# Taking the first feature sums out of PSUM, all on VectorE, and five idle matmuls at the start of a two-branch decoder layer

## The chip, the cores and the metric

The kernel runs on one core of one Trainium2 chip. The metric is the device time of one launch in microseconds. Before the change it is 1397.15 us, the median of three runs (1396.82 to 1398.56). Durations of single instructions come from one profiled execution of the kernel before, taken by the hardware profiler.

## The reference

One decoder layer over 1040 rows of 1024 channels (16 learned tokens ahead of 1024 rows of x), in fp32:

```python
u = rmsnorm(h, mix_norm_pre[l])
proj = u @ w_in[l]
q, f_logit, i_in, g_out, v_pool, gate_a, gate_b = jnp.split(proj, cuts, axis=-1)
a = hgrn2(q, f_logit, i_in, g_out, lbs[l], hgrn_out_norm[l])
p = multiscale_pool(v_pool, pool_proj[l], pool_scale[l])
z = sigmoid(gate_a) * (a @ w_branch_hgrn[l]) + sigmoid(gate_b) * (p @ w_branch_pool[l])
h = h + rmsnorm(z @ w_out[l], mix_norm_post[l])
```

A gated MLP with a depthwise convolution follows. The change touches only the beginning: the norm of the rows, the product for `i_in` (V), the first two products for `g_out` (G), and the operands of the gates' products.

## The kernel before

**Numbers.** Every fp32 product is made of three faster ones. An operand is split into hi (a rounded copy, written by ScalarE) and lo (the rest, a subtraction on VectorE or GpSimd); TensorE adds hi·hi, hi·lo and lo·hi (L160 to L162 for V, L173, L174 and L177 for projections, L262, L263 and L265 for gates).

**Rows to features.** The rows come in nine tiles, in the order 1, 5, 2, 6, 3, 7, 0, 4, 8 of `vtiles` (tile 0 is the 16 learned rows). For each, ScalarE sums squares, VectorE multiplies by the root's reciprocal and the gain (`un`, L352), TensorE transposes 128 columns at a time into a PSUM bank (`pt`, L363), ScalarE copies it to `uhi` (L366) and VectorE subtracts to `ulo` (L368). The gain row itself is spread over the 128 partitions by two fp32 matmuls with a row of ones (`pg`, L437).

**V.** Four weight blocks `wi` are split into hi and lo (`split_wi`, L446 and L447, the lo of the second and fourth on GpSimd). Each tile then takes 24 matmuls. The first two tiles are interleaved by weight block; the later ones run one after the other, with the norm and transposes of later tiles between them.

**G.** Two projections G0 and G1 of 1026 columns in eight k steps of nine matmuls. Their weights are split on ScalarE (L136) and VectorE (L137). A sigmoid on ScalarE (L714) empties their PSUM banks.

**Gates.** The two gate matrices are computed by Strassen's scheme with seven products P1 to P7 for each unit of 256 columns. It takes four quarters of u (b11, b21, b22 and, for the sums, b12) and four sums of them, t1 to t4. With n the number of a row tile, the quarters' columns of tile n go with those of tile n + 4:

- t1 = b12 - b11, t2 = b22 - t1, t3 = t2 - b11, t4 = b21 - t2.

Each sum is made for 128 columns at a time from the hi and lo of `uhi` and `ulo` (`gate_steps`), and then spread, which is to say split again, into its hi (ScalarE, L333) and lo (VectorE, L334) in two halves. `SUMS_AT` says behind which V tile (5 to 8) or around which G projection (9 and more) the next step of which column block is put: block 0 is two columns at the front, blocks 1 to 4 are 128 columns each. A block has three steps: the sums t1 and t2; their spreads and the sums t3 and t4; their spreads.

**Order.** In this part the order on ScalarE, VectorE and TensorE is the written one (`manual_schedule`); GpSimd's is set by the scheduler. Each engine takes its queue strictly in order. The first gate products may begin when the sigmoid of G1 has emptied its banks, since PSUM is then shared out anew.

Of the kernel before, what the change touches and what calls it, by code (L numbers as in the profile page):

```python
# [12 lines left out]
ALU = mybir.AluOpType  # L13

P = 128
D = 1024
SEQ = 1024
NM = 16
# [16 lines left out]
HT = 514  # L35
EARLY = 4
EARLY_G = 2
SUMS_AT = {5: (1,), 6: (1, 2), 7: (1, 2), 8: (3, 2), 9: (3, 4, 0), 10: (3, 4, 0), 11: (4, 0)}
FM_SLOTS = 24
NRAW = 3  # L40
ZA = 4
# [15 lines left out]
def trunk_kernel(ctx: ExitStack, tc: tile.TileContext, x, meta_tokens, mix_norm_pre,  # L57
# [30 lines left out]
    def slot(n, dtype=F32, name="s"):  # L88
        return stage["fm", "p"].tile([P, n], dtype, tag="fm", name=nm(name), padded_shape=[P, L])
# [4 lines left out]
    def bank(name="ps"):  # L94
        return stage["ps", "p"].tile([P, 512], F32, tag="ps", name=nm(name))
# [14 lines left out]
    def rr(a):  # L110
        return a.bitcast(F32)
# [243 lines left out]
    def norm_rows(row, rows, gbc):  # L355
        return list(norm_steps(row, rows, gbc))[-1]

    def feature_steps(un, rows, uhi, ulo, t_at):
        for j in range(2):
            pt = bank("pt")  # L360
            for i in range(4):
                k = 4 * j + i
                pe.transpose(pt[:, i * rows : (i + 1) * rows], un[:rows, k * P : (k + 1) * P], ident[:rows, :rows])  # L363
            src = pt[:, : 4 * rows].rearrange("p (i t) -> p i t", i=4)
            h = uhi[:, 4 * j : 4 * j + 4, t_at : t_at + rows]
            act.copy(h, src)  # L366
            yield
            dve.tensor_tensor(ulo[:, 4 * j : 4 * j + 4, t_at : t_at + rows], src, rr(h), ALU.subtract)  # L368
            yield

    def to_features(*args):
        for _ in feature_steps(*args):
            pass
# [58 lines left out]
    ones1 = slot(P, name="ones1")  # L432
    dve.memset(ones1[:1], 1.0)
    g1 = slot(D, name="g1")
    gps = [bank("pg1") for _ in range(2)]
    for j in range(2):
        pe.matmul(gps[j], ones1[:1], g1row[:1, j * 512 : (j + 1) * 512], start=True, stop=True)  # L437

    wi = []

    def split_wi(raw):
        if len(wi) < 3:
            hi, lo = (wst.tile([P, 1024], F32R, tag=t, name=nm(t)) for t in ("whi", "wlo"))
        else:
            hi, lo = slot(1024, F32R, "wihi"), slot(1024, F32R, "wilo")
        act.copy(hi, raw)  # L446
        (pool_e if len(wi) % 2 else dve).tensor_tensor(lo, raw, rr(hi), ALU.subtract)  # L447
        wi.append((hi, lo))

    def v_mm(ps, t0, k):  # L450
# [12 lines left out]
    uns = {}  # L463

    def v_norm(i):
        if i < len(vtiles):
            uns[i] = norm_rows(rows_in[i], vtiles[i][1], g1)

    def v_feat(i):
        if i < len(vtiles):  # L470
            to_features(uns[i], vtiles[i][1], uhi, ulo, vtiles[i][0])

    vd = dram.tile([NCH, P, 512], F32, name="vscr")
    vmeta = const.tile([P, 512], F32, name="vmeta")
# [352 lines left out]
    def gate_steps(d):  # L827
        a, b = (slice(T0 + d.start + o, T0 + d.stop + o) for o in (0, 512))
        (b11h, b11l), (b21h, b21l), (b12h, b12l), (b22h, b22l) = (
            [rr(u[:, 4 * i : 4 * i + 4, c]) for u in (uhi, ulo)] for i, c in ((0, a), (1, a), (0, b), (1, b)))  # L830
        t1, t2 = halves_tmp(d.stop - d.start)
        pool_e.tensor_tensor(t2, b12l, b11l, ALU.subtract)
        dve.tensor_tensor(t1, b12h, b11h, ALU.subtract)
        dve.tensor_tensor(t1, t1, t2, ALU.add)
        dve.tensor_tensor(t2, b22h, t1, ALU.subtract)
        pool_e.tensor_tensor(t2, t2, b22l, ALU.add)
        yield
        put("t1", t1, d, dve, gq)
        put("t2", t2, d, dve, gq)
        dve.tensor_tensor(t1, t2, b11h, ALU.subtract)  # L840
        pool_e.tensor_tensor(t1, t1, b11l, ALU.subtract)
        dve.tensor_tensor(t2, b21h, t2, ALU.subtract)
        pool_e.tensor_tensor(t2, t2, b21l, ALU.add)
        yield
        put("t3", t1, d, dve, gq)
        put("t4", t2, d, dve, gq)
        yield
# [5 lines left out]
    vb = [bank("pv") for _ in range(2)]  # L853
    E = mybir.EngineType
    with tc.manual_schedule(engines={E.Activation, E.DVE, E.PE}):
        dve.tensor_copy(g1[:, :512], gps[0])
        n0, n1 = (norm_steps(rows_in[i], P, g1) for i in range(2))
        next(n0)
        next(n0)
        dve.tensor_copy(g1[:, 512:], gps[1])  # L860
        un0 = next(n0)
        next(n1)
        f0 = feature_steps(un0, P, uhi, ulo, vtiles[0][0])
        split_wi(raws[0])
        next(f0)
        next(f0)
        next(f0)
        next(n1)
        un1 = next(n1)
        next(f0)  # L870
        v_mm(vb[0], vtiles[0][0], 0)
        v_mm(vb[0], vtiles[0][0], 1)
        split_wi(raws[1])
        f1 = feature_steps(un1, P, uhi, ulo, vtiles[1][0])
        next(f1)
        next(f1)
        split_wi(raws[2])
        next(f1)
        next(f1)
        split_wi(raws[3])  # L880
        for i, j in ((0, 1), (1, 0), (0, 2), (1, 1), (0, 3), (1, 2), (1, 3)):
            for k in (2 * j, 2 * j + 1):
                v_mm(vb[i], vtiles[i][0], k)
        v_norm(2)
        v_norm(3)
        for i in range(2):
            v_feat(2 + i)
            v_norm(4 + i)
        for i in range(2):
            v_out(vb[i], vtiles[i][0])  # L890
        for i in range(2, len(vtiles)):
            ps = bank("pv")
            for k in range(KD):
                v_mm(ps, vtiles[i][0], k)
            if i < 5:
                v_feat(i + 2)
            if i == 5:
                v_feat(7)
                v_feat(8)
            v_norm(i + 4)  # L900
            if i == 3:
                params()
            if i == 5:
                for q in ("t2", "t1", "t3", "t4"):
                    two_halves(q)
                sums = [gate_steps(d) for d in ds]
            if i == len(vtiles) - 1:
                gl = Loader([job("G", h)[:2] + (P,) for h in range(EARLY_G)])
            for j in SUMS_AT.get(i, ()):
                next(sums[j])  # L910
            v_out(ps, vtiles[i][0])
        gates.load_first(0)
        gates.load_first(1)
        gates.ahead(2)
        for h in range(EARLY_G):
            src, n_k, xs, chunks, post = job("G", h)
            r = proj(None, 0, n_k, xs, chunks, ws=gl.next(), name="pg")
            for j in SUMS_AT.get(9 + 2 * h, ()):
                next(sums[j])
            post(r)  # L920
            if h == 0:
                gates.load_first(2)
                gates.ahead(4)
            for j in SUMS_AT.get(10 + 2 * h, ()):
                next(sums[j])

        close_pool("ps")
        open_pool("pf", 4, PSUM)
        gates.load_first(3)
        for e in range(0, EARLY, 2):  # L930
            p = gates.start_pair(e)
            for f in [f[i] for i in range(2) for f in p]:
                f()
                for j in SUMS_AT.get(13, ()) if e == 0 else ():
                    next(sums[j], None)
# [562 lines left out]
```

## Time and profile before

| | |
|---|---|
| median of three runs | 1397.15 us |
| lowest and highest | 1396.82, 1398.56 us |
| the profiled execution | 1396.61 us |
| its span, first to last instruction | 1394.9 us |
| TensorE busy | 1353.6 us, 97% |
| VectorE busy | 973.9 us, 70% |
| ScalarE busy | 565.0 us, 41% |
| GpSimd busy | 508.4 us, 36% |
| mean granted TensorE clock | 0.990 |

In the profile PE is TensorE's matmuls, PEld its weight loads, DVE VectorE, ACT ScalarE, POOL GpSimd. In a timeline a row has the start, the time from there to the end of the last of the instructions that it stands for, engine, line, operation, output and input names, shape and count; what stands in brackets is the idle time before it and the engine that ended it. Matmuls overlap, so a matmul's own time is longer than the distance to the next one. In a table of stretches each engine's busy time has its count of instructions behind it; the last three numbers are the granted clock, the share of the DMA engines' time and GB/s.

### The profile page before, as it was taken

How to read it: one execution, taken by the hardware profiler on the slowest of the kernel's cores; microseconds unless marked ns; L12 is line 12 of the kernel's file. 1: busy time of each engine (PE TensorE's matmuls, PEld its weight loads, DVE VectorE, ACT ScalarE, POOL GpSimd, SP SyncE). 2: the span in 40 equal slices, each digit the busy share in tenths (PEclk: the TensorE clock that was granted, in tenths of full speed). 3: DMA queues.
4: the chain of work that ended last, by engine and by line, in shares of the span. 5: the costliest groups of instructions: out<-in, count | busy, mean ns of one | idle time of the engine just before them, and what ended most of it. 6: DMA issues, size and time to landing. Idle time of an engine off the chain costs nothing. (4 is left out here: it accounts for less than half of the span.)

```text
span 1394.9 us, 21573 instructions
## 1 busy us (share of the span) xinstructions
PE 1353.6 (97%) x8405; PEld 1224.6 (88%) x8405; DVE 973.9 (70%) x1381; ACT 565.0 (41%) x945; POOL 508.4 (36%) x379
## 2 busy tenths in 40 slices
PE   8989999999999999999997999999999999999997
PEld 6879999999999899987777788888999988788786
DVE  6694655288975756565579888888887777654557
ACT  5443333356465463126564322222323223543343
POOL 4255331217543611051036565634567552000100
PEclk9999999999999999999998999999999999999999
DMA  6033433321111023589852577665677879966524
GB/s 245 31 100 121 138 104 108 103 73 46 33 33 33 18 76 122 182 265 316 288 172 91 148 218 214 192 173 145 161 166 188 197 194 268 365 231 201 179 71 166
DMA packets 133220, 215.21 MB, mean 154 GB/s; under 512 B 8327, under 2 KB 76523, under 8 KB 133120
## 3 DMA queue, kind: packets, MB, share of 16 engines
q1 hardware_dynamic: 121056, 189.47, 40.2%
q0 software_dynamic: 12064, 24.38, 10.3%
q8 instruction: 66, 1.08, 0.3%
q14 instruction: 34, 0.28, 0.1%
HBM read 160.84 MB, written 76.05 MB: 170 GB/s over the span
## 5 line engine op out<-in xcount | busy, mean ns | idle before, releaser
L262 PE MATMUL P<-v,whi 128*128 128x258 f32 (+2 forms) x528 | 162.6, 322 | 3.5 <-DVE g L1197 2.5
L263 PE MATMUL P<-v,whi 128*128 128x258 f32 (+2 forms) x528 | 161.6, 320 | 0.0
L265 PE MATMUL P<-v,wlo 128*128 128x258 f32 (+2 forms) x528 | 140.8, 321 | 1.1 <-DVE wlo L210 1.1
L137 POOL TENSOR_TENSOR wlo<-wraw,whi 128x1024 fp32r<-128x1024 f32 (+2 forms) x23 | 50.0, 2174 | 183.0 <-ACT whi L136 101.3
L262 PEld LDWEIGHTS P<-v,whi 128*128 128x128 f32 x528 | 100.8, 191 | 11.8 <-DVE g L1197 2.9
L263 PEld LDWEIGHTS P<-v,whi 128*128 128x128 f32 x528 | 100.7, 191 | 7.5
L161 PE MATMUL pd<-rot 128*128 128x512 f32 x272 | 106.0, 390 | 0.3 <-DVE rot L1257 0.3
L162 PE MATMUL pd<-rot 128*128 128x512 f32 x272 | 105.9, 389 | 0.0
L265 PEld LDWEIGHTS P<-v,wlo 128*128 128x128 f32 x528 | 87.9, 190 | 8.8 <-DVE wlo L210 1.3
L136 ACT CAST whi<-wraw 128x1024 fp32r<-128x1024 f32 (+2 forms) x44 | 36.2, 825 | 146.0 <-PE pba L174 31.3
L209 ACT CAST whi<-wraw 128x512 fp32r<-128x512 f32 x90 | 53.0, 617 | 101.8 <-PE P L263 83.9
L1257 DVE TENSOR_TENSOR rot<-yt,rot 128x1024 fp32r<-128x1024 f32 x33 | 41.2, 1250 | 71.0 <-ACT rot L1256 71.0
L210 DVE TENSOR_TENSOR wlo<-wraw,whi 128x512 fp32r<-128x512 f32 x82 | 75.9, 949 | 18.5 <-ACT whi L209 18.5
L1141 POOL TENSOR_TENSOR ys<-y 128x512 f32<-128x512 f32 x22 | 35.2, 1600 | 142.3 <-issue 96.8
L235 POOL TENSOR_TENSOR swa<-wraw,wraw 128x512 f32<-128x512 f32 x30 | 45.5, 1518 | 95.9 <-DMA wraw<-in_w_in_dram 62.4
L160 PE MATMUL pd<-rot 128*128 128x512 f32 x272 | 72.7, 390 | 2.0 <-ACT rot L1256 2.0
L1256 ACT CAST rot<-yt 128x1024 fp32r<-128x1024 f32 x33 | 34.6, 1053 | 90.2 <-PE pd L161 90.2
L209 ACT CAST whi<-swa 128x512 fp32r<-128x512 f32 x60 | 35.9, 619 | 86.8 <-PE P L263 71.6
L1189 DVE SCALAR_TENSOR_TENSOR y<-g,par,y 128x1024 f32<-128x1024 f32 x44 | 65.1, 1479 | 0.7
L160 PEld LDWEIGHTS pd<-rot 128*128 128x128 f32 x272 | 50.9, 188 | 13.5 <-ACT rot L1256 2.9
L210 DVE TENSOR_TENSOR wlo<-swb,whi 128x512 fp32r<-128x512 f32 x60 | 55.6, 932 | 9.7 <-ACT whi L209 9.4
L209 ACT CAST whi<-swb 128x512 fp32r<-128x512 f32 x60 | 35.9, 618 | 62.9 <-PE P L263 62.0
(344 smaller groups left out, 4320.2 us busy)
## 6 DMA issues: line engine op xcount, KB each, us to landing
wraw<-in_w_in_dram SPq DMA_DIRECT2D x36, 512.0 KB
yt<-ysum SPq DMA_DIRECT2D x33, 512.0 KB
wraw<-in_ffn_w_gate_dram SPq DMA_DIRECT2D x26, 512.0 KB
wraw<-in_w_out_dram SPq DMA_DIRECT2D x24, 512.0 KB
wraw<-in_ffn_w_up_dram SPq DMA_DIRECT2D x22, 512.0 KB
wsum<-in_ffn_w_down_dram SPq DMA_DIRECT2D x22, 512.0 KB
ysum<-ys SPq DMA_DIRECT2D x11, 768.0 KB
sa<-sscr SPq DMA_DIRECT2D x16, 513.0 KB
```

What stands on the lines that cost most here:

```text
L137: eng.tensor_tensor(lo, raw, rr(hi), ALU.subtract)
L160: pe.matmul(ps, ahi, bhi, start=first, stop=False)
L161: pe.matmul(ps, ahi, blo, start=False, stop=False)
L162: pe.matmul(ps, alo, bhi, start=False, stop=last)
L209: act.copy(hi, src)
L210: (pool_e if 4 <= i < 2 * self.early else dve).tensor_tensor(lo, src, rr(hi), ALU.subtract)
L235: pool_e.tensor_tensor(s1, a21, a22, ALU.add)
L262: pe.matmul(x[:, o : o + w], whi[:, k, :], xh[:, c : c + w], start=(k == 0), stop=False)
L263: pe.matmul(x[:, o : o + w], whi[:, k, :], xl[:, c : c + w], start=False, stop=False)
L265: pe.matmul(x[:, o : o + w], wlo[:, k, :], xh[:, c : c + w], start=False, stop=(k == 3))
L1189: dve.scalar_tensor_tensor(a, g[:, :, j : j + n], cvw[:, j, m : m + 1], a, ALU.mult, ALU.add)
L1257: dve.tensor_tensor(lo, src, rr(hi), ALU.subtract)
```

## The change

It has four parts.

- The sums t1 and t2 of blocks 2, 3 and 4 are computed when tiles 6, 7 and 8 leave PSUM: behind each subtraction to `ulo`, VectorE takes the transposed tile itself (not its hi and lo) and subtracts hi and lo of the tile four before (three instructions in place of five). Their step in `gate_steps` then starts with the spread. Blocks 0 and 1 keep the five instructions.
- All instructions of the sums that were on GpSimd are on VectorE, and so are the second and fourth lo of `wi`.
- `SUMS_AT` puts the steps at other places.
- Five matmuls of 128 x 128 x 128 in fp32, of the constant matrix with the identity into a bank that nothing reads (`warm`).

```diff
-SUMS_AT = {5: (1,), 6: (1, 2), 7: (1, 2), 8: (3, 2), 9: (3, 4, 0), 10: (3, 4, 0), 11: (4, 0)}
+SUMS_AT = {5: (2,), 6: (2, 1), 8: (3,), 9: (1, 3), 10: (1, 4), 11: (4, 0), 12: (0, 0)}
...
             dve.tensor_tensor(ulo[:, 4 * j : 4 * j + 4, t_at : t_at + rows], src, rr(h), ALU.subtract)
+            if more:
+                more(j, src)
             yield
...
+    junk_bank = bank("pj")
+
+    def warm(n):
+        for _ in range(n):
+            pe.matmul(junk_bank[:, :P], onesm, ident, start=True, stop=True)
+
+    warm(2)
     gps = [bank("pg1") for _ in range(2)]
...
-        (pool_e if len(wi) % 2 else dve).tensor_tensor(lo, raw, rr(hi), ALU.subtract)
+        dve.tensor_tensor(lo, raw, rr(hi), ALU.subtract)
...
+    t12 = {}
+
+    def sums_of(t0):
+        a = slice(t0 - 512, t0 - 512 + P)
+        t1, t2 = t12[a.start] = halves_tmp(P)
+
+        def more(j, src):
+            if j == 0:
+                dve.tensor_tensor(t1, src, rr(uhi[:, :4, a]), ALU.subtract)
+                dve.tensor_tensor(t1, t1, rr(ulo[:, :4, a]), ALU.subtract)
+            else:
+                dve.tensor_tensor(t2, src, t1, ALU.subtract)
+        return more
...
-            to_features(uns[i], vtiles[i][1], uhi, ulo, vtiles[i][0])
+            t0, rows = vtiles[i]
+            to_features(uns[i], rows, uhi, ulo, t0, sums_of(t0) if t0 >= NM + 5 * P else None)
...
-        t1, t2 = halves_tmp(d.stop - d.start)
-        pool_e.tensor_tensor(t2, b12l, b11l, ALU.subtract)
-        dve.tensor_tensor(t1, b12h, b11h, ALU.subtract)
-        dve.tensor_tensor(t1, t1, t2, ALU.add)
-        dve.tensor_tensor(t2, b22h, t1, ALU.subtract)
-        pool_e.tensor_tensor(t2, t2, b22l, ALU.add)
-        yield
+        if a.start in t12:
+            t1, t2 = t12[a.start]
+        else:
+            t1, t2 = halves_tmp(d.stop - d.start)
+            dve.tensor_tensor(t2, b12l, b11l, ALU.subtract)
...
+            dve.tensor_tensor(t2, t2, b22l, ALU.add)
+            yield
         put("t1", t1, d, dve, gq)
         put("t2", t2, d, dve, gq)
         dve.tensor_tensor(t1, t2, b11h, ALU.subtract)
-        pool_e.tensor_tensor(t1, t1, b11l, ALU.subtract)
+        dve.tensor_tensor(t1, t1, b11l, ALU.subtract)
         dve.tensor_tensor(t2, b21h, t2, ALU.subtract)
-        pool_e.tensor_tensor(t2, t2, b21l, ALU.add)
+        dve.tensor_tensor(t2, t2, b21l, ALU.add)
...
     with tc.manual_schedule(engines={E.Activation, E.DVE, E.PE}):
+        warm(3)
         dve.tensor_copy(g1[:, :512], gps[0])
```

How the instructions move is shown at three places. First TensorE's beginning, before and then changed (`pg` is the spread gain, `pj` the bank that nothing reads, `pt` a bank of transposes, `pv` a V bank):

```order
L437 MATMUL pg_23_128<-g1row_88,ones_21_125 128x512
L437 MATMUL pg_24_129<-g1row_88,ones_21_125 128x512
L363 MATMUL pt_198<-ident,un_178 128x128 x4
L363 MATMUL pt_205<-ident,un_178 128x128 x4
L160 MATMUL pv_172<-whi_194,uhi_86 128x512
```

```order
L442 MATMUL pj_128<-ident,onesm 128x128 x5
L447 MATMUL pg_24_131<-g1row_88,ones1_21_125 128x512
L447 MATMUL pg_25_132<-g1row_88,ones1_21_125 128x512
L363 MATMUL pt_204<-ident,un_184 128x128 x4
L363 MATMUL pt_211<-ident,un_184 128x128 x4
L160 MATMUL pv_175<-whi_200,uhi_86 128x512
```

All five idle matmuls come ahead of the gain's two, though three of them are written behind.

Second, VectorE ahead of the two weight splits of G (`wlo` from `wraw`), before and then changed (`tt` holds t1 and t2 of one block):

```order
L334 TENSOR_TENSOR t2l_578<-tt_121_638,t2h_576 128x2x128
L334 TENSOR_TENSOR t2l_579<-tt_121_638,t2h_577 128x2x128
L840 TENSOR_TENSOR tt_121_638<-tt_121_638,uhi_86 128x512
L842 TENSOR_TENSOR tt_121_638<-uhi_86,tt_121_638 128x512
L137 TENSOR_TENSOR wlo_721<-wraw_718,whi_720 128x1024
L137 TENSOR_TENSOR wlo_727<-wraw_724,whi_726 128x1024
L833 TENSOR_TENSOR tt_132_730<-uhi_86 128x512
```

```order
L861 TENSOR_TENSOR tt_126_658<-ulo_87 128x512
L862 TENSOR_TENSOR tt_126_658<-uhi_86 128x512
L863 TENSOR_TENSOR tt_126_658<-tt_126_658 128x512
L864 TENSOR_TENSOR tt_126_658<-uhi_86,tt_126_658 128x512
L865 TENSOR_TENSOR tt_126_658<-tt_126_658,ulo_87 128x512
L137 TENSOR_TENSOR wlo_721<-wraw_718,whi_720 128x1024
L137 TENSOR_TENSOR wlo_727<-wraw_724,whi_726 128x1024
L334 TENSOR_TENSOR t1l_600<-tt_83_444,t1h_598 128x2x128
```

Before (`tt_121` is block 2, `tt_132` block 3), block 1 is complete ahead of the weights, and block 2 but for its last spreads. Now (`tt_126` is block 1, `tt_83` block 3) block 2 is complete ahead of them, and blocks 1, 3 and 4 have t1 and t2.

Third, ScalarE around the sigmoid that empties G1's banks, before and then changed (`tt_142` and `tt_104` are block 4, `tt_144` and `tt_152` block 0):

```order
L333 CAST t3h_584<-tt_142_844 128x2x128
L333 CAST t3h_585<-tt_142_844 128x2x128
L333 CAST t4h_588<-tt_142_844 128x2x128
L333 CAST t4h_589<-tt_142_844 128x2x128
L333 CAST t3h_584<-tt_144_850 128x2x2
L333 CAST t3h_585<-tt_144_850 128x2x2
L333 CAST t4h_588<-tt_144_850 128x2x2
L333 CAST t4h_589<-tt_144_850 128x2x2
L714 ACTIVATE sg_992<-pg_901 128x342
```

```order
L333 CAST t3h_602<-tt_104_576 128x2x128
L333 CAST t3h_603<-tt_104_576 128x2x128
L333 CAST t4h_606<-tt_104_576 128x2x128
L333 CAST t4h_607<-tt_104_576 128x2x128
L740 ACTIVATE sg_972<-pg_883 128x342
L740 ACTIVATE sg_972<-pg_884 128x342
L740 ACTIVATE sg_972<-pg_885 128x342
L333 CAST t1h_598<-tt_152_966 128x2x2
```

The spreads of block 4 stand ahead of the sigmoid in both; those of block 0 have moved behind it.

More of the change, by code (lines that the diff above doesn't have):

```diff
@@ L356, in norm_rows, with feature_steps @@
         return list(norm_steps(row, rows, gbc))[-1]
-    def feature_steps(un, rows, uhi, ulo, t_at):
+    def feature_steps(un, rows, uhi, ulo, t_at, more=None):
         for j in range(2):
@@ L830, in gate_steps @@
             [rr(u[:, 4 * i : 4 * i + 4, c]) for u in (uhi, ulo)] for i, c in ((0, a), (1, a), (0, b), (1, b)))
-        t1, t2 = halves_tmp(d.stop - d.start)
-        pool_e.tensor_tensor(t2, b12l, b11l, ALU.subtract)
-        dve.tensor_tensor(t1, b12h, b11h, ALU.subtract)
-        dve.tensor_tensor(t1, t1, t2, ALU.add)
-        dve.tensor_tensor(t2, b22h, t1, ALU.subtract)
-        pool_e.tensor_tensor(t2, t2, b22l, ALU.add)
-        yield
+        if a.start in t12:
[3 more added lines that the diff above has]
+            dve.tensor_tensor(t2, b12l, b11l, ALU.subtract)
+            dve.tensor_tensor(t1, b12h, b11h, ALU.subtract)
+            dve.tensor_tensor(t1, t1, t2, ALU.add)
+            dve.tensor_tensor(t2, b22h, t1, ALU.subtract)
+            dve.tensor_tensor(t2, t2, b22l, ALU.add)
+            yield
         put("t1", t1, d, dve, gq)
@@ L909, in trunk_kernel @@
             for j in SUMS_AT.get(i, ()):
-                next(sums[j])
+                next(sums[j], None)
             v_out(ps, vtiles[i][0])
@@ L918, in trunk_kernel @@
             for j in SUMS_AT.get(9 + 2 * h, ()):
-                next(sums[j])
+                next(sums[j], None)
             post(r)
@@ L924, in trunk_kernel @@
             for j in SUMS_AT.get(10 + 2 * h, ()):
-                next(sums[j])
+                next(sums[j], None)
         close_pool("ps")
```

## The prediction

> **What bounds the kernel now.** I read the page first, then busy time by stretches, then TensorE's waits up to 190 us, then the timelines of single engines around each wait. The page's span and engines, and four stretches (start; rest of the V products; the two G projections; first gate products):
>
> ```profile
> span 1394.9 us, 21573 instructions
> PE 1353.6 (97%) x8405; PEld 1224.6 (88%) x8405; DVE 973.9 (70%) x1381; ACT 565.0 (41%) x945; POOL 508.4 (36%) x379
> ```
>
> ```profile
> 0.00:26.00 26.00, 21.28 (x73) 14.37 (x74) 16.41 (x22) 13.07 (x22) 15.06 (x40) 1.00 0.88 307
> 26.00:70.70 44.70, 44.70 (x223) 36.64 (x220) 31.24 (x53) 25.10 (x54) 9.13 (x6) 1.00 0.10 37
> 70.70:102.30 31.60, 25.43 (x145) 24.84 (x144) 31.19 (x53) 14.05 (x41) 17.23 (x13) 0.89 0.31 99
> 102.30:240.00 137.70, 137.63 (x1157) 137.63 (x1158) 70.11 (x95) 47.46 (x85) 49.55 (x36) 1.00 0.36 119
> ```
>
> TensorE (first number) is busy 97% of the span. Before 240 us it loses time only in the first and third stretch; in the third VectorE (third number) is the full engine, and TensorE's granted clock is 0.89. In the second stretch VectorE has 13 us to spare. After 102.3 us TensorE runs without a gap, so a microsecond won before that moves everything behind it. The two longest waits of TensorE up to 190 us (total, times, longest):
>
> ```profile
> PE pg L177 <- DVE wlo L137: 3.6, 1, 3.6
> PE P L262 <- ACT sg L714: 2.7, 1, 2.7
> ```
>
> Both end on engines whose work the change moves; the rest of TensorE's loss is at the start.
>
> **The gate weights (L137).** TensorE's timeline (start, duration; the first row opens the last V tile, an L177 group closes each eighth of a G projection):
>
> ```profile
> 65.02 0.39 PE L160 MATMUL pv<-whi,uhi 128*128 128x512 f32 x1
> ...
> 71.64 0.32 PE L174 MATMUL pg<-ulo,whi 128*128 128x342 f32 x1
> 75.51 1.22 PE L177 MATMUL pg<-uhi,wlo 128*128 128x342 f32 x3 [3.55 <-DVE wlo L137]
> 78.24 1.06 PE L177 MATMUL pg<-uhi,wlo 128*128 128x342 f32 x3
> 80.72 0.62 PE L177 MATMUL pg<-uhi,wlo 128*128 128x342 f32 x3
> 99.08 0.62 PE L177 MATMUL pg<-uhi,wlo 128*128 128x342 f32 x3
> 102.37 0.39 PE L262 MATMUL P<-uhi,whi 128*128 128x258 f32 x1 [2.66 <-ACT sg L714]
> ```
>
> From 80.72 to 99.08 there are 13 eighths, 1.41 us each. The group at 75.51 could have followed 71.64 after 0.16: 71.80, so it is 3.71 late. The next two eighths, 75.51 to 80.72, take 5.21 instead of 2.82: 2.39 lost to the lower clock that follows the gap. Together 6.10.
>
> VectorE's and GpSimd's timelines show why wlo is late:
>
> ```profile
> 28.84 1.42 DVE L352 SCALAR_TENSOR_TENSOR un<-row,rstd,g 128x512 f32<-128x512 f32 x2
> 53.42 2.48 DVE L368 TENSOR_TENSOR ulo<-pt,uhi 128x512 fp32r<-128x512 f32 x4 [2.23 <-ACT uhi L366]
> 61.51 0.68 DVE L840 TENSOR_TENSOR tt<-tt,uhi 128x512 f32<-128x512 f32 x1
> 62.83 1.79 DVE L833 TENSOR_TENSOR tt<-uhi 128x512 f32<-128x512 f32 x1
> 73.17 4.50 DVE L137 TENSOR_TENSOR wlo<-wraw,whi 128x1024 fp32r<-128x1024 f32 x2
> 95.42 0.75 DVE L334 TENSOR_TENSOR t1l<-tt,t1h 128x256 fp32r<-128x256 f32 x2
> ```
>
> ```profile
> 1.27 0.28 POOL masks.py:199 TENSOR_SCALAR_AFFINE_SELECT ident<-ident 128x128 f32<-128x128 f32 x1
> 11.70 2.66 POOL L447 TENSOR_TENSOR wlo<-wiraw,whi 128x1024 fp32r<-128x1024 f32 x1 [2.73 <-ACT whi L446]
> 62.33 1.74 POOL L841 TENSOR_TENSOR tt<-tt,ulo 128x512 f32<-128x512 f32 x1 [1.37 <-DVE tt L840]
> 99.26 1.27 POOL L843 TENSOR_TENSOR tt<-tt,ulo 128x512 f32<-128x512 f32 x1
> ```
>
> A 512-wide sum costs VectorE 0.68 while GpSimd stands idle (61.51) and 1.79 while GpSimd runs one (62.83 against 62.33 to 64.07). The two L137 took 4.50; the same size takes 1.23 undisturbed (row at 9.61 below). So a sum on GpSimd, 1.3 to 1.7 long, costs VectorE about as much as doing it.
>
> Tiles 6 and 7 get their three new sums (2.0 us each) inside the second stretch, where VectorE has room. Then its new queue from the last transposes on (the new sums have the changed file's line numbers), at 0.61 a step (four at 53.42 take 2.48), 0.72 where a step needs the one before, 0.335 for a 256-wide half. Four ulo and block 4's three sums from 53.42, done 57.84; four halves of block 2 59.2; its four sums (L869 to L872) 61.9; four halves 63.25; block 1's five sums (L861 to L865) 66.6. Then wlo, whose whi waits on ScalarE for v_out of the tile that TensorE ends at 65.0: whi by 66.75, wlo 66.8 to 68.0. TensorE wants it at 71.80: 3.8 us of cover, and the wait goes. No transfer is added or moved past another; the gates' next weight loads go out when a wlo has read its buffer, so sooner. I take the whole 6.10; bounds 0 (if all cover is eaten) and 6.10.
>
> **The entry to the gates.** The first gate product needs sigmoid L714 to have emptied a bank. ScalarE's timeline:
>
> ```profile
> 8.53 1.05 ACT L446 CAST whi<-wiraw 128x1024 fp32r<-128x1024 f32 x1 [0.77 <-DMA wiraw<-in_w_in_dram]
> 88.16 1.28 ACT L714 ACT_TABLE_LOAD   x1 [5.04 <-issue]
> 89.46 1.15 ACT L714 ACTIVATE sg<-pg 128x342 f32<-128x342 f32 x3
> 100.56 0.71 ACT L333 CAST t4h<-tt 128x256 fp32r<-128x256 f32 x2 [0.51 <-POOL tt L843]
> 101.87 1.14 ACT L714 ACTIVATE sg<-pg 128x342 f32<-128x342 f32 x3
> ```
>
> The last t4h stands ahead of it and waits for GpSimd's sum of 99.26, done 100.53. With nothing ahead, the first bank is full at 99.08 + 0.32 = 99.40, one sigmoid is 0.4, hand-overs 0.1: entry near 99.95 instead of 102.37. Worth 2.4, if the spread is done in time.
>
> It is, by this count, start as before: G1's last group moves from 99.08 to 92.98 and ends 93.45, G0 eight eighths sooner, 82.15. VectorE after wlo: second wlo 69.2, block 3's halves 70.5 and sums 73.25, P1's two wlo 74.5, block 1's halves 75.8 and sums 78.55, block 3's last halves 79.9. P2's wlo must wait for the sigmoids after G0 (82.15, then 1.28 of table load, 1.15, two casts): 85.0 to 86.2. Then block 1's last halves, block 4's halves and four sums: L872 ends 91.6, t4h 92.35, against 93.45. Cover 1.1 us, behind 5 us of idle. Bounds 0 and 2.4; I take 2.4. The small sums of columns 0 and 1 now stand behind the sigmoid on ScalarE; what they feed is needed eight products later (23 us), so they cost nothing.
>
> **The start.** TensorE again, then VectorE:
>
> ```profile
> 2.44 3.75 PE L437 MATMUL pg<-g1row,ones 1*128 1x512 f32 x4 [2.44 <-DMA g1row<-in_mix_norm_pre_dram]
> 7.63 1.09 PE L363 MATMUL pt<-ident,un 128*128 128x128 f32 x4 [1.45 <-POOL mask L495]
> 12.08 0.63 PE L160 MATMUL pv<-whi,uhi 128*128 128x512 f32 x1
> 14.97 1.00 PE L363 MATMUL pt<-ident,un 128*128 128x128 f32 x4 [0.55 <-DVE un L352]
> 16.50 0.40 PE L160 MATMUL pv<-whi,uhi 128*128 128x512 f32 x1
> 25.52 1.91 PE L363 MATMUL pt<-ident,un 128*128 128x128 f32 x16
> 385.19 0.39 PE L693 MATMUL po<-sc,vh 128*128 128x128 f32 x2
> 385.41 0.39 PE L694 MATMUL po<-qs,st 128*128 128x128 f32 x2
> ```
>
> ```profile
> 9.61 1.23 DVE L447 TENSOR_TENSOR wlo<-wiraw,whi 128x1024 fp32r<-128x1024 f32 x1 [0.66 <-ACT whi L446]
> 11.35 3.56 DVE L352 SCALAR_TENSOR_TENSOR un<-row,rstd,g 128x512 f32<-128x512 f32 x2
> ```
>
> All five idle matmuls stand ahead of the gain's broadcast. At full clock such an fp32 128x128 matmul takes 0.22 (385.19 to 385.41), so 0.45 at half clock: 2.2 us from the identity's end (1.27 + 0.28 on GpSimd), and the broadcast starts near 3.9 instead of 2.44. That makes the second half of the first un about 0.3 late, hidden by wlo, which waits for a transfer until 8.53 + 1.05 anyway. Without that cover it costs 0.3 to 1.5.
>
> The gain comes from un of the second row tile: 3.56 beside GpSimd's L447, 1.42 undisturbed (28.84). So un is ready by 12.8, ulo by 13.4, the second wlo (now VectorE's, 1.2) by 14.6. What TensorE then does depends on its clock: a V product shows 0.63 at 12.08 and 0.40 at 16.50, a transpose 0.27 at 7.63 (four in 1.09) and 0.12 at 25.52 (16 in 1.91). At full speed the last transposes end by 13.4 and TensorE waits for wlo until 14.6: in the old trace the products of that block could start when the transposes of 14.97 ended, near 16.0, so the gain is 1.4. If the clock stays low until then, only the 0.55 of waiting at 14.97 goes, less what the broadcast's push gives back: 0.35. Bounds -0.5 (idle matmuls twice as long: the first un 2.5 late, the second wlo at 16.5) and 1.5; I take 1.2, because a slow clock is needed almost to its old release for less.
>
> The Trainium skill, "TensorE: Matmul & The Clock Gate", Part 1, says that a busy window of some 3.4 us, free-running, lifts the half clock. By it 6 us of unbroken work from 1.6 on would very probably do so before the first V product, and the gain would be 1.4. Here a broadcast of 3.75 us did not lift it, as the transposes of 7.63 show, so the trace leaves it open.
>
> **The sum.** 6.10 + 2.4 + 1.2 = 9.7. The profiled execution took 1396.61 (span 1394.9, 1.7 around it): 1386.9. It lay 0.54 under the median 1397.15, so about 1387.3 for a median.
>
> **Rivals.**
> - *The entry stays late.* If VectorE needs 1.1 us more than counted after G0, the spread again holds the sigmoid; with 3.5 us more all of the 2.4 is gone: up to 1389.8. For it: the cover is short. Against: every duration is from an undisturbed row. 0.12.
> - *The start gives nothing*, since the idle matmuls fill no wait but push the broadcast back, and the clock stays low: minus 0.3 at worst in my count, 1388.8. 0.08.
> - *The gain is absorbed later*, by a wait that does not move with TensorE: near 1396.6. Against: behind the first gate products every engine's order is the old one, and the loads follow TensorE's own progress. 0.04.
> - *VectorE becomes the bound; slower.* From the last transposes to t4h its queue holds 22 sums of two operands in SBUF. If these take 1.7 by themselves, as at 62.83, and not because of GpSimd, 22 more microseconds meet 6.3 of idle and cover: entry near 109.6 instead of 102.37, less 1.2 from the start: 1402.6. It turns slower from 1.45 a sum. Against it: 0.68 at 61.51, with GpSimd idle. 0.04.
>
> **How the numbers follow.** The forecast with all three terms has 0.72: 1387.3, its own range 1385 to 1389.5. The range 1384.5 to 1392 takes in the first two rivals and a first wait only partly removed. A measurement of this kernel can tell 0.2% (2.8 us) from no change: faster 0.91 (forecast and the first two rivals, less 0.01), same 0.05, slower 0.04.
>
> **What would show it.** No wait of the G projection on its wlo, and eighths of 1.41 from the first; VectorE's un of the second tile at 1.4 for two; the first gate product near 92.6 and its wait under 0.6; TensorE without a gap behind it. The forecast is wrong if VectorE's sums stay above 1 us with GpSimd idle, if t4h ends after G's last product, or if the lead at the gates' entry is not there at the end.

## The result, and the profile after

The changed kernel takes 1388.51 us (median of four runs, 1386.93 to 1390.21), the kernel before, run beside it, 1397.86 us (four runs, 1396.82 to 1399.85). The ratio is 0.9933, with a 95% interval of 0.9917 to 0.9950: faster by 9.4 us. The forecast was 1387.3 us.

The profiled execution, the slowest of the four, took 1390.21 us, with a span of 1388.5. From its page, the engines' busy time, and then the same in stretches as before (PE, PEld, DVE, ACT, POOL, then granted clock, DMA share, GB/s):

```profile
PE 1353.9 (98%) x8415; PEld 1225.2 (88%) x8415; DVE 961.7 (69%) x1397; ACT 564.5 (41%) x945; POOL 474.6 (34%) x357
```

```profile
0.00:26.00 26.00, 23.91 (x90) 17.54 (x91) 14.74 (x24) 13.56 (x24) 7.88 (x37) 1.00 0.88 308
26.00:70.70 44.70, 44.70 (x222) 37.01 (x221) 34.33 (x68) 26.14 (x55) 0.00 (x0) 1.00 0.14 51
70.70:102.30 31.60, 31.36 (x220) 31.08 (x218) 19.77 (x55) 15.63 (x44) 3.87 (x3) 1.00 0.32 96
```

In the third stretch TensorE went from 25.43 us busy to 31.36 and its clock from 0.89 to 1.00, VectorE from 31.19 to 19.77. In the second VectorE took 3.1 us more, in the 13 that it had to spare. The 1.00 of the first stretch says nothing, before or after: a trace's record of the clock begins with its first rise to full, at 15.0 us here (V products go from 0.63 to 0.40), and what lies ahead of it is counted as full. TensorE's timeline:

```profile
1.60 2.50 PE L442 MATMUL pj<-ident,onesm 128*128 128x128 f32 x10 [1.60 <-POOL ident masks.py:199]
4.04 3.78 PE L447 MATMUL pg<-g1row,ones 1*128 1x512 f32 x4
7.84 1.09 PE L363 MATMUL pt<-ident,un 128*128 128x128 f32 x4
...
12.09 0.63 PE L160 MATMUL pv<-whi,uhi 128*128 128x512 f32 x1
...
24.77 1.91 PE L363 MATMUL pt<-ident,un 128*128 128x128 f32 x16
...
70.71 0.63 PE L177 MATMUL pg<-uhi,wlo 128*128 128x342 f32 x3
72.13 0.63 PE L177 MATMUL pg<-uhi,wlo 128*128 128x342 f32 x3
...
91.92 0.62 PE L177 MATMUL pg<-uhi,wlo 128*128 128x342 f32 x3
92.78 0.39 PE L262 MATMUL P<-uhi,whi 128*128 128x258 f32 x1 [0.23 <-ACT sg L740]
```

G's wait on wlo is gone (70.71 has no bracket), eighths take 1.41 from the first, and the first gate product comes at 92.78 in place of 102.37: a lead of 9.59. Of it 0.75 was there at the third row tile's transposes (24.77 for 25.52). VectorE and ScalarE show why:

```profile
11.36 1.41 DVE L352 SCALAR_TENSOR_TENSOR un<-row,rstd,g 128x512 f32<-128x512 f32 x2
...
66.88 1.22 DVE L137 TENSOR_TENSOR wlo<-wraw,whi 128x1024 fp32r<-128x1024 f32 x1 [1.14 <-ACT whi L136]
...
88.59 0.69 DVE L872 TENSOR_TENSOR tt<-tt,ulo 128x512 f32<-128x512 f32 x1
```

```profile
89.37 0.71 ACT L333 CAST t4h<-tt 128x256 fp32r<-128x256 f32 x2 [0.62 <-DVE tt L872]
92.27 1.15 ACT L740 ACTIVATE sg<-pg 128x342 f32<-128x342 f32 x3 [2.19 <-PE pg L177]
...
712.70 1.06 ACT L1148 ACTIVATE un<-m 114x1024 f32<-114x1024 f32 x1
...
720.39 0.62 ACT L209 CAST whi<-wraw 128x512 fp32r<-128x512 f32 x1 [5.25 <-DMA wraw<-in_ffn_w_gate_dram]
```

The first weight split ends at 68.10, 2.6 us ahead of TensorE's need (70.71); the last t4h ends at 90.08, 2.19 before the sigmoid.

**Where 3.2 us of the lead went in this execution.** The spans differ by 6.4 only. Matching the TensorE instructions of the two traces one by one gives the lead of the changed kernel along the way (place in the time of before):

| place, us | 115 | 300 | 600 | 690 | 720 | 780 | 815 | 850 | 1385 |
|---|---|---|---|---|---|---|---|---|---|
| lead, us | 9.53 | 9.24 | 8.84 | 9.17 | 8.75 | 7.24 | 7.06 | 6.39 | 6.38 |

It is carried nearly whole to 720 and then falls, in the entry to the MLP. The same two ScalarE rows in the trace of before:

```profile
721.52 1.06 ACT L1118 ACTIVATE un<-m 114x1024 f32<-114x1024 f32 x1
...
727.26 0.63 ACT L209 CAST whi<-wraw 128x512 fp32r<-128x512 f32 x1 [3.29 <-DMA wraw<-in_ffn_w_gate_dram]
```

At 712.70 the lead is 8.82; the split behind waits 5.25 us for its transfer in place of 3.29, and the lead is 6.87. The next norm stands behind that split on ScalarE. The profiles put this down to the execution and not to the change: in the twelve kernels below the lead changed between 600 and 850 by anything from +0.4 to -3.9 us (median -0.4), against this one profile of before; e3 and e4, whose code behind the gates is the changed kernel's, lost nothing there (+0.1). The runs of one kernel lie 1.5 to 8.5 us apart, and half a microsecond is read from landmarks of the trace, not from the times.

### The profile page after: what moved, and what is told of

Its sections match the earlier page's. It is cut to its first block, busy times and chain, and to the rows that moved or that the text cites. A ratio compares the mean times of both kernels' runs of the same rounds, so it can differ in the third digit from the quotient of the medians.

```text
span 1388.5 us, 21566 instructions
## 1 busy us (share of the span) xinstructions
PE 1353.9 (98%) x8415; PEld 1225.2 (88%) x8415; DVE 961.7 (69%) x1397; ACT 564.5 (41%) x945; POOL 474.6 (34%) x357
## 5 line engine op out<-in xcount | busy, mean ns | idle before, releaser
L262 PEld LDWEIGHTS P<-v,whi 128*128 128x128 f32 x528 | 100.9, 191 | 15.5 <-DVE g L1227 4.9
L262 PE MATMUL P<-t2h,whi 128*128 128x258 f32 (+1 forms) x196 | 58.0, 312 | 3.7 <-ACT t2h L333 2.8
```

Source lines behind the costliest of these rows:

```text
L262: pe.matmul(x[:, o : o + w], whi[:, k, :], xh[:, c : c + w], start=(k == 0), stop=False)
```

## The experiments

Times are medians of the number of runs in brackets, ratios are to runs of before on the same chip (medians 1397.4 to 1398.1). Then three landmarks of the profile: the third row tile's transposes, G's wait on wlo, and the first gate product.

| kernel | us (runs) | ratio, 95% | transposes | G's wait | gate product |
|---|---|---|---|---|---|
| before | 1397.86 (4) | 1 | 25.52 | 3.55 | 102.37 |
| changed | 1388.51 (4) | 0.9933, 0.9917 to 0.9950 | 24.77 | 0 | 92.78 |
| e1_no_idle | 1387.84 (4) | 0.9928, 0.9910 to 0.9946 | 23.96 | 0 | 92.31 |
| e2_vector_only | 1390.13 (4) | 0.9947, 0.9927 to 0.9967 | 25.12 | 1.52 | 94.52 |
| e3_sums_gpsimd | 1387.26 (4) | 0.9930, 0.9913 to 0.9948 | 24.34 | 0 | 92.40 |
| e4_wi_gpsimd | 1387.65 (4) | 0.9936, 0.9915 to 0.9957 | 25.52 | 0 | 93.56 |
| e5_idle_behind | 1387.96 (4) | 0.9925, 0.9910 to 0.9939 | 24.72 | 0 | 92.33 |
| e6_entry6 | 1390.37 (4) | 0.9956, 0.9938 to 0.9973 | 23.82 | 0 | 93.94 |
| e7_wlo_late9 | 1392.60 (10) | 0.9967, 0.9954 to 0.9981 | 24.74 | 2.59 | 95.63 |
| e8_wlo_late14 | 1397.79 (10) | 1.0007, 0.9994 to 1.0020 | 24.94 | 6.24 | 100.89 |
| e9_bank_before | 1394.94 (10) | 0.9982, 0.9972 to 0.9991 | 24.92 | 3.55 | 98.20 |
| e10_vector_bank | 1389.72 (4) | 0.9938, 0.9921 to 0.9954 | 25.70 | 1.52 | 96.99 |
| e11_wi_only | 1396.08 (10) | 0.9991, 0.9979 to 1.0003 | 25.75 | 3.53 | 102.54 |
| e12_no_idle_bank | 1387.41 (5) | 0.9938, 0.9921 to 0.9956 | 24.14 | 0 | 91.79 |

### Which half carries the gain: VectorE alone, or three sums out of PSUM and new places

**e2_vector_only**, the kernel before with all gate sums on VectorE:

```diff
-        pool_e.tensor_tensor(t2, b12l, b11l, ALU.subtract)
+        dve.tensor_tensor(t2, b12l, b11l, ALU.subtract)
...
```

> The kernel before with nothing changed but the sums of the gates' operands, which all go to VectorE, five and four instructions a block, at their old places. Theory (GpSimd's part is one half, the three sums in place of five and the new places the other): VectorE's queue from 55.8 is 18 sums of 0.68 and 12 halves of 0.335 long, so the two weight splits start near 72.4, the first ends near 73.7 at 1.23; TensorE waits 2 us in place of 3.6 and keeps its clock (eighths of 1.41 behind it), so 4 of the 6.1 us are gained; the last t4h is still late, and the first gate product comes near 97.6 (102.37 before, 92.78 in the changed kernel); time near 1392.5. Rival A (GpSimd alone was the cause): first gate product 93 to 94, time 1388 to 1389. Rival B (a sum beside GpSimd's costs VectorE as much as doing that one too, so nothing is gained): first gate product 101 to 102.5, time 1396 to 1397.5.

TensorE of this kernel, then ScalarE:

```profile
72.74 0.73 PE L177 MATMUL pg<-uhi,wlo 128*128 128x342 f32 x3 [1.52 <-DVE wlo L137]
...
94.52 0.28 PE L262 MATMUL P<-uhi,whi 128*128 128x258 f32 x1
```

```profile
94.52 0.71 ACT L333 CAST t4h<-tt 128x256 fp32r<-128x256 f32 x2 [0.61 <-DVE t1l L334]
...
95.52 1.13 ACT L714 ACTIVATE sg<-pg 128x342 f32<-128x342 f32 x3
```

The wait on wlo shrank to 1.52, near the 2 expected. But the first gate product came three microseconds early, and *before* the sigmoid of G1 had even begun: it cannot have waited for it. By the waits written into the program (the trace shows only that it did not wait), its bank was last emptied by a sigmoid of G0, whereas in the kernel before it was the first sigmoid of G1. Nothing in the edit touches banks; the allotment of PSUM to tiles came out another way. So this run does not say what VectorE alone does at the entry; e10 below does.

**e3_sums_gpsimd**, the changed kernel with the old sharing of the sums:

```diff
-            dve.tensor_tensor(t2, b12l, b11l, ALU.subtract)
+            pool_e.tensor_tensor(t2, b12l, b11l, ALU.subtract)
...
-        dve.tensor_tensor(t2, t2, b21l, ALU.add)
+        pool_e.tensor_tensor(t2, t2, b21l, ALU.add)
```

> The changed kernel with the sums of gate_steps shared with GpSimd as they were before (the second and fourth of the four, the first and last of the five); what is taken out of PSUM, the new places, the start and the idle matmuls stay. Theory (three sums out of PSUM and the new places carry most): a sum beside GpSimd's goes to 1.7 us and the weight splits to 2.2, but the first still ends by 70.5, before TensorE wants it at 70.7: no wait of the G projection above 0.5; the last t4h comes 1.5 to 2.5 us later than in the changed kernel and meets the sigmoid's cover of 2.2; first gate product 92.8 to 94, time 0 to 1.5 us above the changed kernel's. Rival (GpSimd's presence on the port is what costs): first weight split later than 72, a wait of G of 2 us or more, first gate product 96 or later, time 3 us or more above the changed kernel's.

VectorE and ScalarE of this kernel:

```profile
66.50 3.35 DVE L137 TENSOR_TENSOR wlo<-wraw,whi 128x1024 fp32r<-128x1024 f32 x2 [0.25 <-ACT whi L136]
```

```profile
90.01 0.71 ACT L333 CAST t4h<-tt 128x256 fp32r<-128x256 f32 x2 [0.53 <-POOL tt L872]
91.89 1.15 ACT L740 ACTIVATE sg<-pg 128x342 f32<-128x342 f32 x3 [1.17 <-PE pg L177]
```

The two splits take 3.35 beside GpSimd in place of 2.4, and the cover at the entry falls from 2.19 to 1.17, by less than the 1.5 to 2.5 expected; neither cover is used up, the first gate product comes at 92.40, and the time is the changed kernel's (1387.26). With three sums out of PSUM and the new places, GpSimd's share costs nothing: those two carry the whole gain of G and the entry by themselves. No run parts one of them from the other. VectorE alone would bring a part of the same gain, so the two halves do not add.

### The entry: late spread, or the bank

**e10_vector_bank**, e2 with one spare PSUM bank taken at the start:

```diff
+    for _ in range(1):
+        dve.memset(bank("pj")[:1, :1], 0.0)
     gps = [bank("pg1") for _ in range(2)]
```

> The kernel before with all gate sums on VectorE (where the first gate product came at 94.52 without a wait, because its bank was one of G0's), and one spare bank taken at the start, by which the first gate product inherits the bank of G1's second sigmoid. Theory (with the bank as it was the last t4h would still be late): sigmoids of G1 from 95.5 as there, the second done near 96.3, first gate product near 96.4, with a wait for ScalarE of 1.8; time 1.9 us above that kernel's 1390.1. Rival (the work on VectorE, not the bank, freed the entry): first gate product at 94.5 to 95.

Its TensorE, then ScalarE:

```profile
94.68 0.62 PE L177 MATMUL pg<-uhi,wlo 128*128 128x342 f32 x3
96.99 0.38 PE L262 MATMUL P<-uhi,whi 128*128 128x258 f32 x1 [1.68 <-ACT sg L716]
```

```profile
95.15 0.71 ACT L333 CAST t4h<-tt 128x256 fp32r<-128x256 f32 x2 [0.62 <-DVE t1l L334]
...
96.15 1.13 ACT L716 ACTIVATE sg<-pg 128x342 f32<-128x342 f32 x3
```

The wait is back, as expected: 1.68 on a t4h that is still late. With a bank of G1 (here that of the second sigmoid, 0.4 behind the first), VectorE alone brings the first gate product to 96.99: 5.4 of the 9.6 us. In the time the 1.9 expected does not show (1389.72 against e2's 1390.13; each is known to some 2 us).

**e9_bank_before**, the kernel before with four spare banks (the same lines with `range(4)`):

> The kernel before with four spare banks taken at the start, each touched by a one-element memset of VectorE, and nothing else. That turns the sharing out of PSUM round: the first gate product now inherits a bank that a sigmoid of G0 emptied, in place of the first sigmoid of G1. Theory (the wait of 2.66 at the entry was for that bank alone): G's wait on wlo stays at 3.6, the first gate product follows G's last matmul at 99.6 (102.37 before), time 2.7 us shorter than before: 1394.5. Rival (the spread of t4 on ScalarE holds the gates in any case, through the sigmoids or the weights): first gate product 101 or later, time as before.

Its TensorE:

```profile
74.87 0.79 PE L177 MATMUL pg<-uhi,wlo 128*128 128x342 f32 x3 [3.55 <-DVE wlo L137]
77.17 1.06 PE L177 MATMUL pg<-uhi,wlo 128*128 128x342 f32 x3
79.34 0.64 PE L177 MATMUL pg<-uhi,wlo 128*128 128x342 f32 x3
...
97.73 0.63 PE L177 MATMUL pg<-uhi,wlo 128*128 128x342 f32 x3
98.20 0.28 PE L262 MATMUL P<-uhi,whi 128*128 128x258 f32 x1
...
102.46 0.39 PE L262 MATMUL P<-uhi,whi 128*128 128x258 f32 x1 [1.25 <-ACT sg L716]
```

The first gate product follows G's last matmul directly. Part of this is given back at 102.46, where the next product needs a bank of G1 and the late t4h holds it for 1.25. The time is 2.8 us below before (0.9982, interval below 1), about the 2.7 expected, though in the profile 0.6 of the lead is the start's and 0.7 a shorter loss of clock, and the entry's net share is 1.4.

**e6_entry6**, the changed kernel with six more sums ahead of the last t3h and t4h:

```diff
-        dve.tensor_tensor(t1, t2, b11h, ALU.subtract)
+        for _ in range(7 if d.start == HALO + 3 * P else 1):
+            dve.tensor_tensor(t1, t2, b11h, ALU.subtract)
```

> The changed kernel with the first of block 4's four sums done seven times over: 6 more VectorE instructions of 0.61 to 0.72, 3.7 to 4.3 us, ahead of the last t3h and t4h on ScalarE. Theory (the cover at the entry is the 2.2 us that ScalarE stands idle between the last t4h, done at 90.06, and G1's sigmoid): t4h ends at 93.8 to 94.4, the sigmoid follows, and the first gate product comes 0.5 behind at 94.3 to 94.9 (92.78), with a wait for ScalarE of 1.8 to 2.4; time 1.5 to 2.1 above the changed kernel's. Rival (the cover is the 1.1 us of the prediction's count): 95.4 to 96.

Its ScalarE, then TensorE (each row opens a group of six products):

```profile
92.82 0.71 ACT L333 CAST t4h<-tt 128x256 fp32r<-128x256 f32 x2 [0.62 <-DVE tt L873]
93.43 1.14 ACT L740 ACTIVATE sg<-pg 128x342 f32<-128x342 f32 x3
```

```profile
93.94 0.39 PE L262 MATMUL P<-uhi,whi 128*128 128x258 f32 x1 [2.30 <-ACT sg L740]
...
95.11 0.42 PE L262 MATMUL P<-uhi,whi 128*128 128x258 f32 x1
...
96.39 0.42 PE L262 MATMUL P<-uhi,whi 128*128 128x258 f32 x1
...
97.68 0.31 PE L262 MATMUL P<-uhi,whi 128*128 128x258 f32 x1
```

The first gate product comes at 93.94 with a wait of 2.30; this execution's start was 0.95 earlier (transposes at 23.82), so that is 94.9 on the changed kernel's scale, the upper end of what was expected. The sums made t4h 4.4 us later and the wait 2.1 longer: the cover is 2.3. Time 1.9 us above the changed kernel's, in the expected 1.5 to 2.1. But this execution lost more than the wait: behind it the three groups took 3.74 us, where the changed kernel's take 2.25 (92.78 to 95.03), at a granted clock of 0.50 from 94.3 to 97.7. The wait of 2.30 so cost 1.49 to the clock, which the expectation did not have; that the time fits all the same may be luck, or other executions kept the clock. This stays open.

### The price of G's wait, and the clock

**e8_wlo_late14** and **e7_wlo_late9** put sums of no use ahead of G's weight splits (15 and 10 in the place of one):

```diff
-            dve.tensor_tensor(t2, b12l, b11l, ALU.subtract)
+            for _ in range(15 if d.stop - d.start == P else 1):
+                dve.tensor_tensor(t2, b12l, b11l, ALU.subtract)
```

> The changed kernel with one 512-wide sum of block 1 done fifteen times over, ahead of the two weight splits of G: 14 more VectorE instructions of 0.61 to 0.68, 8.5 to 9.5 us. The first split then ends at 68.1 + 8.5 to 9.5 - 1.14 of idle time: 75.5 to 76.5, and TensorE, which wants it at 70.7, waits 4.8 to 5.8 us. Theory (a long gap also drops TensorE's clock, which cost 2.39 before): the next eighths of G take 1.2 to 2.4 us more than 1.41 each in all, and the first gate product comes at 92.78 + 4.8 to 5.8 + 2.4 = 100 to 101; time 7.2 to 8.2 above the changed kernel's. Rival (the slow eighths before were VectorE's weight split and not the clock): 97.6 to 98.6, time 4.8 to 5.8 above.

TensorE of e8:

```profile
77.33 1.22 PE L177 MATMUL pg<-uhi,wlo 128*128 128x342 f32 x3 [6.24 <-DVE wlo L137]
80.06 0.82 PE L177 MATMUL pg<-uhi,wlo 128*128 128x342 f32 x3
81.66 0.63 PE L177 MATMUL pg<-uhi,wlo 128*128 128x342 f32 x3
...
100.89 0.39 PE L262 MATMUL P<-uhi,whi 128*128 128x258 f32 x1 [0.24 <-ACT sg L740]
```

A wait of 6.24, longer than the 4.8 to 5.8 worked out (an added sum took 0.72), and behind it eighths of 2.73 and 1.60: 1.51 lost to the clock. The first gate product comes at 100.9, 8.1 late, and the time is 1397.79, 9.3 above the changed kernel's (7.2 to 8.2 expected). With nothing changed but this wait, which is 2.7 longer than that of the kernel before, the changed kernel is as slow as that one.

> The changed kernel with the first sum of block 1 done ten times over ahead of G's two weight splits: 9 more VectorE instructions of 0.72 (the 14 of the longer version moved the split from 65.74 to 76.05). The first split then ends near 73.4 and TensorE, which wants it at 70.7, waits 2.7 us. What is open is when a gap costs clock: after 1.5 us the next eighths lost 0.1, after 3.55 they lost 1.65 to 2.39, after 6.2 they lost 1.5. Theory (any gap well over 1.5 costs the clock for the same stretch behind it): 1.5 to 2.4 lost, first gate product at 97 to 98. Rival (the clock holds through 2.7 us): at most 0.2 lost, first gate product near 95.6.

TensorE of e7:

```profile
73.46 0.74 PE L177 MATMUL pg<-uhi,wlo 128*128 128x342 f32 x3 [2.59 <-DVE wlo L137]
74.98 0.63 PE L177 MATMUL pg<-uhi,wlo 128*128 128x342 f32 x3
...
95.63 0.39 PE L262 MATMUL P<-uhi,whi 128*128 128x258 f32 x1 [0.24 <-ACT sg L740]
```

The rival held: after 2.59 us the next eighth takes 1.52, 0.11 lost, and the gate product comes at 95.63, 2.85 late. The time is 4.1 above the changed kernel's, 1.2 more than this delay; the profile cannot say why, since it lost 3.9 of its lead between 600 and 850.

### The start

**e1_no_idle** leaves out `warm(2)` and `warm(3)`.

> The changed kernel without its five idle matmuls. Theory (they lifted nothing: in the changed kernel four transposes still took 1.09 us at 7.84 and six V products 3.2 us from 10.15): the gain's broadcast goes back to 2.44, the second row tile's un is unchanged at 1.4 for two, the transposes of the third row tile stay at 24.8 within 0.3 us (24.77 with the idle matmuls), the first gate product at 92.8 within 0.3, the time within 0.5 us of the changed kernel's 1388.5. Rival (the idle matmuls bring the full clock forward by about a microsecond, and carry the start's gain): third tile's transposes at 25.3 to 25.5, first gate product at 93.4, time 0.6 us longer.

**e4_wi_gpsimd** puts the second and fourth lo of the V weights back:

```diff
-        dve.tensor_tensor(lo, raw, rr(hi), ALU.subtract)
+        (pool_e if len(wi) % 2 else dve).tensor_tensor(lo, raw, rr(hi), ALU.subtract)
```

> The changed kernel with the second and fourth lo of the V weights back on GpSimd. Theory (this move is the start's whole gain): the second row tile's two un take 3.5 us again, the third row tile's transposes come at 25.5 (25.52 before, 24.77 in the changed kernel), first gate product near 93.5, time 0.7 us above the changed kernel's. Rival (the idle matmuls carry it): un slow, but transposes at 24.8 to 25.0 and first gate product at 92.8 to 93.0.

**e11_wi_only** is the same line the other way round, alone, in the kernel before.

> The kernel before with the second and fourth lo of the V weights on VectorE, and nothing else. Theory (this is the start's whole gain, 0.8 us on the mean of the profiles so far): the second row tile's two un take 1.4 in place of 3.56, the products of its block start near 14.4 to 15 and the third row tile's transposes at 24.0 to 24.9 (24.92 to 25.70 in four profiles with 3.5); G's wait on wlo stays 3.6 and moves with it, first gate product near 101.5, time 0.8 below before's. Rival (VectorE is the full engine from 53 us on and takes the gain back, since its queue does not start sooner): transposes early, first gate product at 102.2 or later.

**e5_idle_behind** writes the gain's two matmuls into the ordered part and three idle ones behind them:

```diff
-    warm(2)
...
     with tc.manual_schedule(engines={E.Activation, E.DVE, E.PE}):
+        for j in range(2):
+            pe.matmul(gps[j], ones1[:1], g1row[:1, j * 512 : (j + 1) * 512], start=True, stop=True)
         warm(3)
```

> The changed kernel with its idle matmuls behind the gain's broadcast in place of ahead of it, three in place of five. The first gate product then inherits PSUM banks that a sigmoid of G0 emptied, not one of G1. Theory (the idle matmuls ahead only push the broadcast back; the clock rises when it does): broadcast at 2.4, third row tile's transposes at 24.0 (23.96 without idle matmuls, 24.77 in the changed kernel), within 0.4 us; no wait of the first gate product for ScalarE, so it follows G's last matmul at 91.6 (92.31 without idle matmuls, 92.78 changed); time about 1 us below the changed kernel's. Rival (unbroken full-width work from 6.2 us on lifts the clock sooner): the V products of 12 us at 0.40 in place of 0.63 and the transposes at 23.6 or earlier. Rival on the entry (the spread, not the bank, sets it): first gate product 0.2 to 0.6 behind G's last all the same.

**e12_no_idle_bank** is e5 without idle matmuls and with five spare banks.

> The changed kernel without idle matmuls, and with five spare banks taken at the start (one-element memsets on VectorE), by which the first gate product inherits a bank that a sigmoid of G0 emptied. Theory (idle matmuls do nothing but can hold the broadcast back; the entry waits for the bank alone): broadcast near 2.4, transposes of the third row tile at 24.0 to 24.8, first gate product right behind G's last matmul at 91.5 to 92.3 without a wait for ScalarE, time 0.4 to 1.2 us below the changed kernel's 1388.5, the lowest of all. Rival (the clock needs the idle matmuls): transposes at 25 or later and first gate product at 92.6 or later.

e4 did as expected in the trace: un 3.54, transposes at 25.52, gate product 93.56; its time, 1387.65, is not above the changed kernel's. e5 missed: its transposes came at 24.72 and not at 24.0, though its gate product followed G's last matmul without a wait, as expected of its bank. e1 looked like a third answer: everything 0.8 *earlier* without the idle matmuls. e11 looked like the opposite: no gain at all. VectorE of e11, and then TensorE of e11 and of e12:

```profile
11.67 1.40 DVE L352 SCALAR_TENSOR_TENSOR un<-row,rstd,g 128x512 f32<-128x512 f32 x2
```

```profile
13.68 1.91 PE L363 MATMUL pt<-ident,un 128*128 128x128 f32 x8
...
75.66 1.22 PE L177 MATMUL pg<-uhi,wlo 128*128 128x342 f32 x3 [3.53 <-DVE wlo L137]
78.39 1.05 PE L177 MATMUL pg<-uhi,wlo 128*128 128x342 f32 x3
```

```profile
13.39 1.12 PE L363 MATMUL pt<-ident,un 128*128 128x128 f32 x8
...
91.32 0.63 PE L177 MATMUL pg<-uhi,wlo 128*128 128x342 f32 x3
91.79 0.28 PE L262 MATMUL P<-uhi,whi 128*128 128x258 f32 x1
```

Two things vary from execution to execution, with or without the edits. The first V weight block lands early or late: its split on ScalarE starts at 7.69 in e1, 7.83 in e6, and between 8.21 and 8.88 in the other profiles. And TensorE's clock rises at a time of its own, from 12.4 us (e6) to 16.8 (e11) in the fourteen traces: the eight transposes of the second row tile take 1.03 us in e6, 1.12 in e12, 1.91 in e11. Counted from that split to the third tile's transposes, the five kernels with the lo on GpSimd took 16.6 to 17.1 (mean 16.8), the nine with it on VectorE 15.6 to 16.9 (mean 16.1). So the move is worth 0.7 on the mean of profiles. By four of them it is worth more when the clock rises early: 1.0 between e4 and e3 (16.6 and 15.6, clock up at 13.3 and 13.6), 0.4 between before and e8 (17.0 and 16.6, clock up at 15.7 and 15.6). Among the nine, the five with idle matmuls ahead have a mean of 16.1, e5 16.0, the three without 16.3: no effect of the idle matmuls can be told apart. The clock rose at 14.1 on the mean of the six profiles with idle matmuls ahead (12.4 to 15.6) and at 15.0 in the seven without (13.6 to 16.8), so a small one stays open. e11's 1396.08 (0.9991, interval across 1) leaves the start's gain open in the time.

(e1's gate product waits 0.58 at the entry: by the program, without the bank of the idle matmuls it inherits that of G1's second sigmoid.) e12 has the earliest gate product, 91.79, behind G's last matmul without a wait. Its 1387.41 was expected to be the lowest time of all; e3's is 1387.26, and neither is told apart from the changed kernel's.

## Why the prediction was right, and where it was not

**The gate weights, 6.10: right.** The wait is gone and eighths are 1.41; matched through the traces, the lead grew by 6.07 there. The first split was expected at 66.8 and came at 66.88, but this agreement is in part luck: the work ahead ran 0.8 earlier than in the count, which took the start as before, and VectorE then stood idle for 1.14, waiting for whi from ScalarE. So the cover was 2.6 and not 3.8. e7 and e8 show the causal half: put back, a wait of 2.59 makes the first gate product 2.85 late, one of 6.24 makes it 8.1 late. What was sized from one sample was the clock's part. 2.39 in the profile of before is 1.65 in e9, 1.51 in e8, and 2.80 in e11 (its rows above: eighths of 2.73, 2.57 and 1.73 from 75.66 on).

**Why the split comes early: counted together, and not needed together.** The prediction took GpSimd's sums as slowing VectorE by what they save. Between 53.4 and 90.0 VectorE is busy 32.6 us for 52 instructions in e3 and 32.3 for 64 in the changed kernel, so that holds there. But it did not ask whether one half of the change would do. Three sums out of PSUM and the new places do all of it (e3); VectorE alone does 5.4 of 9.6 (e10).

**The entry, 2.4: right in size, and incomplete.** The first gate product was put near 92.6 and came at 92.78. The cover was 2.2, not 1.1: L872 ended at 89.3, not 91.6. The step "the first gate product needs sigmoid L714 to have emptied a bank" took for granted which bank that is, as the description of the kernel before does. e9 shows that the allotment alone can take the wait away, e10 beside e2 that one bank more can bring it back; the changed kernel kept a bank of G1, so the early t4h is what paid there (e6).

**The start, 1.2: mis-sized.** The mechanism stands (un 3.56 to 1.41), but the profiled pair shows 0.75 and the mean of profiles 0.7. The step that failed is "a slow clock is needed almost to its old release for less": the clock did stay low that long, to 15.0 in the changed kernel's profile and 15.7 in that of before. The working behind it, more with an early clock and less with a late one, is what the profiles show (1.0 and 0.4 above).

The Trainium skill, "TensorE: Matmul & The Clock Gate", Part 1, would have had the clock up after some 3.4 us of work. Here TensorE worked without a gap from 1.60 to 8.93, up to 7.82 on idle matmuls and the broadcast from one row, and V products at 12.09 still took 0.63; the trace does not agree for this mixture. That page also says that the window runs free, so that the moment varies, by 500 ns either way. Here it does vary, but by 3.2 us over the five traces with the changed kernel's own start (12.4 in e6, 15.6 in e8).

**Rivals.** "The entry stays late" fell: the last t4h ended 2.19 ahead of the sigmoid. "The start gives nothing" fell in the profiles (0.7) and is open in the times. "VectorE becomes the bound" fell: its sums take 0.69 at 88.59. "The gain is absorbed later" fell on the medians (9.35 us between them); in the profiled pair 3.2 were lost behind the gates' entry, 2.5 of them behind 600 us, which the profiles put down to the execution. The sum, 9.7 for a measured 9.35, is closer than its parts, and that is luck: of the 9.59 at the first gate product 0.8 is the start's, 6.07 G's wait and clock, 2.4 the entry, and 0.3 was in no term (G's first products follow the last V product sooner, by 0.23 in place of 0.43 and 0.16 in place of 0.26).

## What to carry to other kernels

Before splitting work anew between two engines, ask which half of the edit reaches the deadline: here fewer sums and better places did, and taking GpSimd out of the sums added nothing to them. Where a stage begins by sharing out PSUM anew, look which earlier tile's bank the first product inherits; spare banks moved its wait by 1.7 us (one bank, e10) and 2.7 (four, e9). And a gain of half a microsecond at the start of a program cannot be read from one pair of profiles when a transfer's landing (1.2 us here) and the clock's rise (4.4) each vary by more.

## What was not expected of the hardware

- Gaps of 3.53 to 6.24 us in TensorE's work ahead of G's split cost it 1.5 to 2.8 us afterwards, gaps of 1.52 (e2) and 2.59 (e7) 0.11. The Trainium skill, "TensorE: Matmul & The Clock Gate", "Why this matters for your kernels", warns of gaps above some 3 us; these agree, but e6 does not: its gap of 2.30 at the entry cost 1.49, while one of 2.66 at the entry of before cost nothing that shows in its rows. So the length of a gap alone does not decide, and what does stays open.
- The cost does not grow with the gap: 2.39 after 3.55 us in before, 2.80 after 3.53, 1.65 after 3.55, 1.51 after 6.24. The granted clock is 0.50 for 6.8 us in before (from 73.8), e11 and e8, and for 3.4 us in e9 and e6, and TensorE loses about half of the time that it works in them: 5.1 us in before, 6.0 in e11, 3.1 in e8, 3.4 in e9 and e6. The part of a slow stretch in which TensorE still waits costs nothing more.
- Unbroken work of TensorE from 1.60 us on is not shown to bring the full clock sooner than work from 2.3 to 2.5 on: the means are 14.1 and 15.0, but single profiles of each spread over more than 3 us.
- The same transfer of an MLP weight block kept ScalarE waiting 3.29 us in one profile and 5.25 in another; over the profiles of thirteen kernels the lead over before changes by up to 4 us in that part of the program.
